# More seven-product pairs in two feed-forward networks, and late ones in their first groups

## The chip, the cores and the metric

The kernel runs on one core of a Trainium2 chip. The metric is the device time of one execution in microseconds (us), lower is better. TensorE (PE in the profile) does matrix products, VectorE (DVE) and ScalarE (ACT) elementwise work, GpSimd (POOL) and SyncE (SP) issue most of the transfers; all of them run their own instructions in order and wait for each other by semaphores.

## The reference

Two transformer blocks for 256 tokens of width 2048, all in float32. Both end in a feed-forward network (FFN), and only these are touched:

```
# block 1: gated, FFN_HIDDEN = 5632
gate, up = split(h @ w_ffn_in)            # 2048 -> 2 x 5632
x = x + rms_norm((silu(gate) * up) @ w_ffn_out, g)
# block 2: squared relu, D_FF = 8192
f = square(relu(x @ w_ff1)) @ w_ff2       # 2048 -> 8192 -> 2048
x = layer_norm(alpha * x + f, g, b)
```

## The kernel before

Every float32 operand is used as two parts, a rounded one (`h` for weights, `H` for activations) and the rest (`l`, `L`). A product of two tiles is three matmuls: high by high, high by low, low by high. Weights stream from memory in halves of 128 x 1024 (SyncE issues the loads, up to five ahead). For each half ScalarE copies it into the rounded part (L253) and VectorE subtracts to get the rest (L254); the pair of tiles (h, l) is one *unit*. Five units fit in the pool, and `Stream.half` asks for the splits four units ahead of TensorE's use. So the split of a unit waits until TensorE has finished the unit five before it.

The contraction over 2048 rows goes in eight *pairs* of 2 x 128 rows. In the first FFN product of both blocks (all but the opening step, `i0`) `Prog.seven` computes a group of 256 tokens x 1024 columns at a time, four blocks of 128 tokens x 512 columns. A string of eight letters says how each pair is done:

- an **N** pair does the eight tile products directly: two units, 24 matmuls into four accumulators `c`;
- an **S** pair does seven products (Strassen-Winograd): four units, 21 matmuls into `c` and four further accumulators `m`. It needs sums of weight tiles, which `splitting4` makes on VectorE (L275, L277, L278) with four splits (L272 on ScalarE, L279 on VectorE), and sums of token tiles, made once per FFN by `seven_gen` beside the opening step.

Before the first S pair of a group takes its accumulators, all delayed work (`late`: transposes and splits of earlier results) is issued at once. After the last S pair ScalarE and VectorE combine `m` into the shared sums (L644 to L651), one part after each of the next two units; at the end of the group L655 adds `c`, and the activation follows: in block 1 L1719 and L1721 (silu, and the product of gate and up), in block 2 L1964 and L1965. The results are then transposed on TensorE (L1750) and split into the hidden operand (L665, L666). These transposes are delayed by one or more units.

The steps run in a fixed order. In block 1 step `i0` is a plain product, `i1`, `i2`, `i3` and `i5` consist of two groups one right behind the other, `i4` of one: nine groups. Where two groups follow each other, the second has its `c` in the banks that the first used for `m`, and the reverse. In block 2 `i1` to `i7` are one group each: seven groups. Between them stand the steps `o`, the second FFN product (L506 to L508). Each `o` step handles the hidden part made one `i` step earlier; `i1` directly follows `i0`.

PSUM is held as two pools: `pa` (three banks) and `pb` (five). In block 2 a group has its `c` in `pb`, three of its `m` in `pa` and one in `pb`, so one bank of `pb` is free for transposes until the first S pair. The `o` step accumulates in `pa`.

The lines named by the prediction: L606 to L608 are the three matmuls of `prod` in `seven`; L506 to L508 those of `rowsmm`; L579 to L584 the token sums.

Of the kernel before, what the change touches and what calls it, by code (L numbers as in the profile page):

```python
# [23 lines left out]
FFN = 5632  # L24
# [13 lines left out]
FF_PARTS = (8,) * 8  # L38
SEQ_GLU = "NSNNSNNN"
SEQ_FF = "NSNSNSNN"  # L40
MID = 64 + 2 + 128
# [34 lines left out]
def _fours():  # L76

    at = lambda i, seq: [i + 2 * p for p, s in enumerate(seq) if s == "S"]
    u, n = [], 0
    for step in FFN_ORDER:  # L80
        nt = FFN_PARTS[int(step[1:])]
        if step[0] == "i" and step != "i0":
            for b in range(nt // 4):
                u += at(n + 16 * b, SEQ_GLU)
        n += 4 * nt if step[0] == "i" else 2 * nt
    n += MID
    for step in FF_ORDER:
        if step[0] == "i" and step != "i0":
            u += at(n, SEQ_FF)
        n += 16  # L90
    return [i - n for i in u]


def _weights(a):
    w_in, w_out = a["w_in"][0], a["w_out"][0]
    w_ckv, w_fi, w_fo = a["w_ckv"][0], a["w_ffn_in"][0], a["w_ffn_out"][0]
# [13 lines left out]
    for step in FFN_ORDER:  # L110
        p = int(step[1:])
        lo, hi = int(starts[p]), int(starts[p + 1])
        if step[0] == "o":
            u.append(_rows(w_fo[lo * 128:hi * 128]))
        elif p == 0:
            u.append(gate_up[lo // 4:hi // 4].reshape(-1, 128, 2048))
        else:
            for b in range(lo * 128, hi * 128, 512):
                u.append(_seven(np.concatenate([w_fi[:, i + b:i + b + 512] for i in (0, FFN)], axis=1), SEQ_GLU))
    u += [  # L120
# [10 lines left out]
    for step in FF_ORDER:  # L131
        p = int(step[1:])
        lo, hi = int(starts[p]), int(starts[p + 1])
        if step[0] == "o":
            u.append(_rows(w2[lo * 128:hi * 128]))
        else:
            u.append(_seven(w1[:, lo * 128:hi * 128], SEQ_FF) if p else _rows(w1[:, lo * 128:hi * 128]))
    w = np.concatenate(u, axis=0)
# [185 lines left out]
class Prog:  # L324
# [243 lines left out]
    def seven_gen(self, xp, seq, st):  # L568


        nc = self.nc
        for i, p in enumerate(p for p, s in enumerate(seq) if s == "S"):
            yield 1.9
            if i % 2 == 0:
                t = self.slot([128, 2, 2, 4, 128], "seven", F32R)
            w = self.t4([128, 2, 4, 128], "s7")
            a = w[:, 0].rearrange("p (k x) t -> p k (x t)", k=2)
            s = w[:, 1]
            nc.vector.tensor_tensor(a, xp.H(2 * p, 2).bitcast(F32), xp.L(2 * p, 2).bitcast(F32), OP.add)  # L579
            a11, a21, a12, a22 = a[:, 0, :128], a[:, 0, 128:], a[:, 1, :128], a[:, 1, 128:]  # L580
            nc.vector.scalar_tensor_tensor(out=s[:, 0], in0=a21, scalar=-1.0, in1=a22, op0=OP.mult, op1=OP.subtract)
            nc.vector.scalar_tensor_tensor(out=s[:, 1], in0=s[:, 0], scalar=-1.0, in1=a11, op0=OP.mult, op1=OP.subtract)
            nc.vector.tensor_tensor(s[:, 2], a11, a21, OP.subtract)
            nc.vector.tensor_tensor(s[:, 3], a12, s[:, 1], OP.subtract)  # L584
            yield 0.7
            self.split2(s, t[:, i % 2, 0], t[:, i % 2, 1])
            st.append(t[:, i % 2])

    def seven(self, xp, seq, st, out, swap=False):
# [22 lines left out]

        si = 0
        for p, s in enumerate(seq):
            if s == "N":
# [7 lines left out]
                continue  # L623
            if si == 0:
                while self.late:
                    self.settle()
                m = {i: f() for i, f in zip((5, 7, 6, 1), more)}
            sum_ = lambda i: (st[si][:, 0, i], st[si][:, 1, i])
            cut = lambda i: slice(512 * i, 512 * i + 512)
# [7 lines left out]
            self.tick()  # L637
            si += 1
            if not end:
# [1031 lines left out]
    def ffn(self):  # L1671
# [4 lines left out]
        hid = {}  # L1676
        g = self.row(2)
        ss = self.cp.tile([128, 2, 8], F32, tag="ss", name="ss2")
        sv, st, after_swap = [], [], False
        last = len(FFN_PARTS) - 1  # L1680
        for step in FFN_ORDER:
            p = int(step[1:])
            nt = FFN_PARTS[p]
            if step[0] == "i":
                hid[p] = Pair(self, "hid", nt)
                if p == 0:
                    self.rowsmm(hT, 16, nt // 2, self.ev_glu(hid[p]), lag=4, begin=lambda: sv.append(self.start(self.seven_gen(hT, SEQ_GLU, st))))
                    continue
                self.drain(sv[0])
                for b in range(nt // 4):  # L1690
                    self.seven(hT, SEQ_GLU, st, self.glu(hid[p], b), swap=b % 2 == 1)
                after_swap = nt == 8
                continue
            if p == last:
                self.xT = Pair(self, "xT2", 16)
# [239 lines left out]
    def ff2(self):  # L1935
        nc, x = self.nc, self.x
        hT = self.hT

        hid, sg, st = {}, [], []
        self.bn = self.cp.tile([128, 2, 8, 6], F32, tag="bn", name="bn1")  # L1940
        last = len(FF_PARTS) - 1
        for step in FF_ORDER:
            p = int(step[1:])
            nt = FF_PARTS[p]
            if step[0] == "i":
# [11 lines left out]
                if p == 0:  # L1957
                    self.rowsmm(hT, 16, nt // 4, ev, lag=4, begin=lambda: sg.append(self.start(self.seven_gen(hT, SEQ_FF, st))))
                    continue
# [8 lines left out]

                self.seven(hT, SEQ_FF, st, relu2)
                continue  # L1970
# [78 lines left out]
```

## Time and profile before

| | |
|---|---|
| median of three runs | 2594.05 us (2592.15 to 2597.99) |
| the profiled execution: its time | 2596.54 us |
| its span in the trace | 2594.8 us |
| TensorE busy, matmuls | 2561.9 us, 12936 |
| VectorE busy | 1786.2 us |
| ScalarE busy | 1325.9 us |
| mean granted TensorE clock | 0.995 |
| seven-product groups of block 1 | 677 to 1241 us, with the `o` steps between |
| seven-product groups of block 2 | 1924 to 2492 us, with the `o` steps between |

In a row of a timeline the first number is the start and the second the duration, both in us, then engine, line and operation, what is written and read, and the number of instructions merged into the row. A bracket at the end is the idle time of that engine just before, with the instruction that ended it. Matmuls overlap each other: a duration of 0.39 us is not the distance between two starts.

### The profile page before, as it was taken

The page shows a single profiled execution, that of the slowest core. Times are in us where ns is not written, and L with a number is a line of the kernel's source. Part 1 is how long each engine was busy: PE and PEld are TensorE (multiplying, and loading weights), DVE is VectorE, ACT ScalarE, POOL GpSimd, SP SyncE. Part 2 cuts the span into 40 slices and gives each one's busy share as a digit, 9 for nine tenths or more (in the row PEclk, how much of TensorE's full clock was granted, in tenths as well). Part 3 has the DMA queues.
Part 4 walks back from the last instruction along what each step waited for, and adds up shares of the span by engine and source line. Part 5 has one row for each costly group of instructions (what it writes and reads, how often), then busy time and mean ns, then how long its engine had stood idle before and what let it go on. Part 6 is the DMA issues. An engine that isn't in the chain of part 4 may idle for free. (4 is left out here: it accounts for less than half of the span.)

```text
span 2594.8 us, 33924 instructions
## 1 busy us (share of the span) xinstructions
PE 2561.9 (99%) x12936; PEld 2171.5 (84%) x12936; DVE 1786.2 (69%) x2270; ACT 1325.9 (51%) x1777; POOL 62.4 (2%) x59
## 2 busy tenths in 40 slices
PE   9999999999999999999999999999999999999998
PEld 8989888988888888888888888888778888888886
DVE  5766857766676767668676764456677776777676
ACT  6533667656455545445444464444445544554553
POOL 0000000110000000000010000000100000000001
PEclk9999999999999999999999999999999999999999
DMA  7544557555555556556555655565456555655663
GB/s 283 179 153 142 176 178 247 196 177 174 192 194 191 198 194 197 194 177 212 188 182 184 208 171 187 195 223 182 152 167 210 195 194 179 205 198 187 216 208 122
DMA packets 134083, 493.34 MB, mean 190 GB/s; under 512 B 15149, under 2 KB 15541, under 8 KB 131744
## 3 DMA queue, kind: packets, MB, share of 16 engines
q1 hardware_dynamic: 129888, 470.34, 53.9%
q0 software_dynamic: 2880, 17.76, 2.1%
q10 hardware_dynamic: 1152, 3.07, 0.3%
q8 instruction: 101, 1.65, 0.3%
q14 instruction: 62, 0.51, 0.1%
HBM read 486.91 MB, written 2.11 MB: 188 GB/s over the span
## 5 line engine op out<-in xcount | busy, mean ns | idle before, releaser
L254 DVE TENSOR_TENSOR l<-w,h 128x1024 fp32r<-128x1024 f32 (+1 forms) x802 | 975.3, 1223 | 669.6 <-ACT h L253 659.0
L253 ACT ACTIVATE h<-w 128x1024 fp32r<-128x1024 f32 (+1 forms) x805 | 844.9, 1058 | 752.0 <-PE pa L508 442.0
L506 PE MATMUL pa<-h,hid 128*128 128x512 f32 (+1 forms) x808 | 316.4, 392 | 0.0
L508 PE MATMUL pa<-h,hid 128*128 128x512 f32 (+1 forms) x808 | 313.1, 388 | 0.0
L507 PE MATMUL pa<-l,hid 128*128 128x512 f32 (+1 forms) x808 | 312.7, 387 | 0.0
L606 PE MATMUL pb<-h,hT 128*128 128x512 f32 x669 | 260.9, 390 | 2.8 <-DVE hid L666 2.8
L608 PE MATMUL pb<-h,hT 128*128 128x512 f32 x669 | 260.5, 389 | 0.0
L607 PE MATMUL pb<-l,hT 128*128 128x512 f32 x669 | 260.4, 389 | 0.0
L506 PE MATMUL pa<-h,xT 128*128 128x512 f32 x500 | 201.6, 403 | 2.5 <-ACT ghg L935 1.3
L508 PE MATMUL pa<-h,xT 128*128 128x512 f32 x500 | 195.7, 391 | 0.0
L507 PE MATMUL pa<-l,xT 128*128 128x512 f32 x500 | 195.5, 391 | 0.0
L508 PEld LDWEIGHTS pa<-h,hid 128*128 128x128 f32 x808 | 151.7, 188 | 31.4
L507 PEld LDWEIGHTS pa<-l,hid 128*128 128x128 f32 x808 | 151.9, 188 | 30.1
L506 PEld LDWEIGHTS pa<-h,hid 128*128 128x128 f32 x808 | 151.8, 188 | 29.7
L606 PEld LDWEIGHTS pb<-h,hT 128*128 128x128 f32 x669 | 125.6, 188 | 28.9 <-DVE hid L666 3.3
L608 PEld LDWEIGHTS pb<-h,hT 128*128 128x128 f32 x669 | 125.6, 188 | 26.2
L607 PEld LDWEIGHTS pb<-l,hT 128*128 128x128 f32 x669 | 125.6, 188 | 25.9
L463 PE MATMUL pa<-xT,h 128*128 128x256 f32 x496 | 142.8, 288 | 1.0 <-ACT xT L685 0.9
L465 PE MATMUL pa<-xT,l 128*128 128x256 f32 x496 | 141.2, 285 | 1.0 <-DVE l L254 1.0
L464 PE MATMUL pa<-xT,h 128*128 128x256 f32 x496 | 141.4, 285 | 0.1
L459 PE MATMUL pa<-xT,h 128*128 128x512 f32 x384 | 134.0, 398 | 0.0
L506 PEld LDWEIGHTS pa<-h,xT 128*128 128x128 f32 x500 | 94.4, 189 | 25.3 <-issue 2.7
(507 smaller groups left out, 4569.6 us busy)
## 6 DMA issues: line engine op xcount, KB each, us to landing
w<-W SPq DMA_DIRECT2D x889, 512.0 KB, 3.5
row<-rows POOLq DMA_DIRECT2D x7, 1024.0 KB, 7.1
xn<-x ACTq DMA_DIRECT2D x2, 1024.0 KB, 8.6
mn<-mem POOLq DMA_DIRECT2D x2, 1024.0 KB, 6.0
memraw<-memT POOLq DMA_DIRECT2D x2, 1024.0 KB, 6.7
x<-x POOLq DMA_DIRECT2D x2, 1024.0 KB, 7.2
xraw<-xT SPq DMA_DIRECT2D x3, 512.0 KB, 8.5
out<-x SPq DMA_DIRECT2D x6, 256.0 KB, 2.5
```

The costliest lines, as they stand in the source:

```text
L253: nc.scalar.activation(out=h[:, s], in_=t[:, s], func=AF.Copy)
L254: (nc.gpsimd if j in self.slow else nc.vector).tensor_tensor(l[:, s], t[:, s], h[:, s].bitcast(F32), OP.subtract)
L459: mm(o, h[:, k], xp.both(kt), start=kt == 0, stop=kt == nkt - 1)
L463: mm(o, h[:, k], xp.H(kt), start=kt == 0, stop=False)
L464: mm(o, h[:, k], xp.L(kt), start=False, stop=False)
L465: mm(o, l[:, k], xp.H(kt), start=False, stop=kt == nkt - 1)
L506: mm(o, xh, h[:, k, c], start=kt == 0, stop=False)
L507: mm(o, xh, l[:, k, c], start=False, stop=False)
L508: mm(o, xl, h[:, k, c], start=False, stop=kt == nkt - 1)
L606: mm(o, ah, wh, start=first, stop=False)
L607: mm(o, ah, wl, start=False, stop=False)
L608: mm(o, al, wh, start=False, stop=end)
```

## The change

The strings become tables with an entry for the first group of an FFN and one for the others. Block 1: `NSNNSNNN` becomes `NSNSNSNN`, and `NNNSNSNN` in the first group. Block 2: `NSNSNSNN` becomes `SNSNSNSN`, and `NNNNSNSN` in the first group. Token sums are kept by the number of their pair (a first group uses some of them only), three pairs in block 1 and four in block 2, where there were two and three. The packing of the weights follows the strings. In block 1 the third tile for token sums takes a slot of 8 KB a partition, and the load of the row `g` (POOL's queue) moves from the start of the FFN to step `o4`.

```diff
-SEQ_GLU = "NSNNSNNN"
-SEQ_FF = "NSNSNSNN"
+SEQ_GLU = {"first": "NNNSNSNN", "": "NSNSNSNN"}
+SEQ_FF = {"first": "NNNNSNSN", "": "SNSNSNSN"}
 ...
     def seven_gen(self, xp, seq, st):
 ...
-            st.append(t[:, i % 2])
+            st[p] = t[:, i % 2]
 ...
     def seven(self, xp, seq, st, out, swap=False):
 ...
-            if si == 0:
+            if not m:
                 while self.late:
                     self.settle()
                 m = {i: f() for i, f in zip((5, 7, 6, 1), more)}
-            sum_ = lambda i: (st[si][:, 0, i], st[si][:, 1, i])
+            sum_ = lambda i: (st[p][:, 0, i], st[p][:, 1, i])
 ...
     def ffn(self):
 ...
-        g = self.row(2)
 ...
                 for b in range(nt // 4):
-                    self.seven(hT, SEQ_GLU, st, self.glu(hid[p], b), swap=b % 2 == 1)
+                    self.seven(hT, SEQ_GLU["first" if p == 1 and b == 0 else ""], st, self.glu(hid[p], b), swap=b % 2 == 1)
 ...
+            if p == last - 1:
+                g = self.row(2)
 ...
     def ff2(self):
 ...
-                self.seven(hT, SEQ_FF, st, relu2)
+                self.seven(hT, SEQ_FF["first" if p == 1 else ""], st, relu2)
```

In the new file the lines of `Stream` up to L600 or so are two further down and those behind `seven` one further (L254 becomes L256, L1750 becomes L1751); L644 to L655 keep their numbers.

What moves, in the order in which the engines run it. TensorE at the first group of block 2, before: behind the first N pair's last matmul both blocks of transposes (`ident,sq`, results of the opening product) stand back to back, and the S pair (its operand `seven` are the token sums) follows.

```order
L608 MATMUL pb_16443<-h_16377,hT_891_15307 128x512
L1750 MATMUL pb_16478<-ident,sq_16434 128x128 x4
L1750 MATMUL pb_16485<-ident,sq_16436 128x128 x4
L606 MATMUL pb_16495<-h_16395,hT_891_15307 128x512
L607 MATMUL pb_16495<-l_16396,hT_891_15307 128x512
L608 MATMUL pb_16495<-h_16395,hT_891_15307 128x512
L606 MATMUL pb_16441<-h_16395,seven_16185 128x512
```

TensorE at the same place after the change, around the second block of transposes (the first stands twelve matmuls ahead):

```order
L608 MATMUL pb_16536<-h_16484,hT_909_15396 128x512
L609 MATMUL pb_16536<-l_16485,hT_909_15396 128x512
L610 MATMUL pb_16536<-h_16484,hT_909_15396 128x512
L1751 MATMUL pb_16601<-ident,sq_16522 128x128 x4
L608 MATMUL pb_16535<-h_16504,hT_909_15396 128x512
L609 MATMUL pb_16535<-l_16505,hT_909_15396 128x512
```

The two blocks now lie a unit apart and have matmuls of N pairs on both sides.

VectorE between the two groups of step `i2` in block 1, before: the shared sums (L645 to L651) with the splits of the next group's N pair among and behind them, then the first sum of weights for its S pair (L275).

```order
L645 TENSOR_TENSOR u_499_7846<-pa_7678,u_498_7845 128x512
L646 TENSOR_TENSOR u_500_7847<-pa_7676,u_499_7846 128x512
L254 TENSOR_TENSOR l_7873<-w_7812,h_7872 128x1024
L650 TENSOR_TENSOR u_499_7846<-pa_7677,u_499_7846 128x512
L651 TENSOR_TENSOR u_501_7848<-pa_7676,u_499_7846 128x512
L254 TENSOR_TENSOR l_7893<-w_7824,h_7892 128x1024
L254 TENSOR_TENSOR l_7911<-w_7836,h_7910 128x1024
L275 TENSOR_TENSOR s_7930<-w_7849,w_7870 128x1024
```

VectorE at the same place after the change:

```order
L645 TENSOR_TENSOR u_504_7909<-pa_7695,u_503_7908 128x512
L646 TENSOR_TENSOR u_505_7910<-pa_7693,u_504_7909 128x512
L256 TENSOR_TENSOR l_7936<-w_7875,h_7935 128x1024
L650 TENSOR_TENSOR u_504_7909<-pa_7694,u_504_7909 128x512
L651 TENSOR_TENSOR u_506_7911<-pa_7693,u_504_7909 128x512
L277 TENSOR_TENSOR s_7957<-w_7887,w_7899 128x1024
```

The shared sums stand two splits later, directly ahead of the S pair's weight sums.

VectorE at the end of a group in block 2 reads the same before and after (five splits, L645, L646, a split, L650, L651, then the splits of the next step), but two of the five splits belonged to the second N pair behind the last S pair, and now belong to the next `o` step.

More of the change, by code (lines that the diff above doesn't have):

```diff
@@ L76, in _fours @@
 def _fours():
+    first = lambda c: "first" if c else ""
     at = lambda i, seq: [i + 2 * p for p, s in enumerate(seq) if s == "S"]
@@ L83, in _fours @@
             for b in range(nt // 4):
-                u += at(n + 16 * b, SEQ_GLU)
+                u += at(n + 16 * b, SEQ_GLU[first(step == "i1" and b == 0)])
         n += 4 * nt if step[0] == "i" else 2 * nt
@@ L88, in _fours @@
         if step[0] == "i" and step != "i0":
-            u += at(n, SEQ_FF)
+            u += at(n, SEQ_FF[first(step == "i1")])
         n += 16
@@ L118, in _weights @@
             for b in range(lo * 128, hi * 128, 512):
-                u.append(_seven(np.concatenate([w_fi[:, i + b:i + b + 512] for i in (0, FFN)], axis=1), SEQ_GLU))
+                s = SEQ_GLU["first" if b == lo * 128 and p == 1 else ""]
+                u.append(_seven(np.concatenate([w_fi[:, i + b:i + b + 512] for i in (0, FFN)], axis=1), s))
     u += [
@@ L136, in _weights @@
         else:
-            u.append(_seven(w1[:, lo * 128:hi * 128], SEQ_FF) if p else _rows(w1[:, lo * 128:hi * 128]))
+            u.append(_seven(w1[:, lo * 128:hi * 128], SEQ_FF["first" if p == 1 else ""]) if p else _rows(w1[:, lo * 128:hi * 128]))
     w = np.concatenate(u, axis=0)
@@ L611, in tok @@
             return tuple(f(kt, 1, tb * 128, tb * 128 + 128) for f in (xp.H, xp.L))
-        si = 0
         for p, s in enumerate(seq):
@@ L637, in seven @@
             self.tick()
-            si += 1
             if not end:
@@ L1676, in ffn @@
         hid = {}
-        g = self.row(2)
         ss = self.cp.tile([128, 2, 8], F32, tag="ss", name="ss2")
-        sv, st, after_swap = [], [], False
+        sv, st, after_swap = [], {}, False
         last = len(FFN_PARTS) - 1
@@ L1686, in ffn @@
                 if p == 0:
-                    self.rowsmm(hT, 16, nt // 2, self.ev_glu(hid[p]), lag=4, begin=lambda: sv.append(self.start(self.seven_gen(hT, SEQ_GLU, st))))
+                    self.rowsmm(hT, 16, nt // 2, self.ev_glu(hid[p]), lag=4, begin=lambda: sv.append(self.start(self.seven_gen(hT, SEQ_GLU[""], st))))
                     continue
@@ L1937, in ff2 @@
         hT = self.hT
-        hid, sg, st = {}, [], []
+        hid, sg, st = {}, [], {}
         self.bn = self.cp.tile([128, 2, 8, 6], F32, tag="bn", name="bn1")
@@ L1957, in ff2 @@
                 if p == 0:
-                    self.rowsmm(hT, 16, nt // 4, ev, lag=4, begin=lambda: sg.append(self.start(self.seven_gen(hT, SEQ_FF, st))))
+                    self.rowsmm(hT, 16, nt // 4, ev, lag=4, begin=lambda: sg.append(self.start(self.seven_gen(hT, SEQ_FF[""], st))))
                     continue
```

## The prediction, made before the changed kernel ran

> **What bounds the kernel now.** I read the page's head first, then TensorE's rows in order of time, then the stretches of time by group, and last VectorE's rows around the edited pairs.
>
> ```profile
> span 2594.8 us, 33924 instructions
> PE 2561.9 (99%) x12936; PEld 2171.5 (84%) x12936; DVE 1786.2 (69%) x2270; ACT 1325.9 (51%) x1777; POOL 62.4 (2%) x59
> L606 PE MATMUL pb<-h,hT 128*128 128x512 f32 x669 | 260.9, 390 | 2.8 <-DVE hid L666 2.8
> row<-rows POOLq DMA_DIRECT2D x7, 1024.0 KB, 7.1
> ```
>
> TensorE is busy for 99% of the span, so a matmul that disappears is worth time only if TensorE is truly fed there. The 390 ns of the matmul's row is not that worth: matmuls overlap. The price is the distance between starts. These are the first matmuls of an S pair, of the S pair two pairs later, and of the N pair behind it, in block 2's second seven-product group:
>
> ```profile
> 2021.82 0.39 PE L606 MATMUL pb<-h,hT 128*128 128x512 f32 x1
> ...
> 2032.02 0.39 PE L606 MATMUL pb<-h,hT 128*128 128x512 f32 x1
> ...
> 2036.78 0.39 PE L606 MATMUL pb<-h,hT 128*128 128x512 f32 x1
> ```
>
> From 2021.82 to 2032.02 TensorE issues one S pair (21 matmuls) and one N pair (24): 10.20 us / 45 = 0.2267 us a matmul. The S pair alone takes 2036.78 - 2032.02 = 4.76 us = 21 x 0.2267, an N pair 10.20 - 4.76 = 5.44 us. Nothing is lost between matmuls. Priced by the row's mean the change would look 1.7 times as large.
>
> The groups as stretches (TensorE, weight load, VectorE, ScalarE, POOL, clock, DMA share, GB/s):
>
> ```profile
> 677.10:764.90 87.80, 86.39 (x389) 71.41 (x388) 65.90 (x70) 44.34 (x48) 0.00 (x0) 1.00 0.56 193
> 939.10:1024.30 85.20, 85.20 (x381) 70.63 (x381) 64.53 (x68) 43.39 (x46) 0.00 (x0) 1.00 0.60 199
> ...
> 1923.60:1970.90 47.30, 44.47 (x193) 36.34 (x192) 34.94 (x38) 23.79 (x26) 0.00 (x0) 0.96 0.54 184
> 2016.30:2057.80 41.50, 41.50 (x185) 34.37 (x184) 33.32 (x35) 22.23 (x23) 0.00 (x0) 1.00 0.61 208
> 2450.90:2492.40 41.50, 41.50 (x185) 34.35 (x183) 33.33 (x35) 22.24 (x23) 0.53 (x1) 1.00 0.71 242
> ```
>
> Rows two, four and five are ordinary: a double gate/up group (85.2 us) and single groups of block 2 (41.5 us), TensorE without a gap. Rows one and three are the first group of each FFN; they alone hold idle TensorE time (1.4 and 2.8 us), and row three has a clock of 0.96.
>
> **The change part by part.** *Matmuls removed.* Gate/up has nine groups. The first keeps two S pairs, the other eight go from two to three. Block 2 has seven: the first goes from three to two, six from three to four. That is 8 + 6 - 1 = 13 more S pairs, 39 fewer matmuls; the built program has just 39 fewer rows on TensorE. 39 x 0.2267 = 8.84 us less, if the operands arrive in time.
>
> *VectorE's added work.* It must hide behind TensorE. One N pair, one S pair, the end of a group on VectorE, and the first matmul of the output product behind it:
>
> ```profile
> 2033.37 2.58 DVE L254 TENSOR_TENSOR l<-w,h 128x1024 fp32r<-128x1024 f32 x2 [0.97 <-ACT h L253]
> 2035.87 1.22 DVE L275 TENSOR_TENSOR s<-w,w 128x1024 f32<-128x1024 f32 x1
> ...
> 2041.91 0.69 DVE L279 TENSOR_TENSOR l<-w,h 128x512 fp32r<-128x512 f32 x1
> 2043.57 6.39 DVE L254 TENSOR_TENSOR l<-w,h 128x1024 fp32r<-128x1024 f32 x5 [0.98 <-ACT h L253]
> 2049.88 0.69 DVE L645 TENSOR_TENSOR u<-pa,u 128x512 f32<-128x512 f32 x1
> ...
> 2052.37 0.68 DVE L650 TENSOR_TENSOR u<-pa,u 128x512 f32<-128x512 f32 x1
> 2053.09 0.69 DVE L651 TENSOR_TENSOR u<-pa,u 128x512 f32<-128x512 f32 x1
> ...
> 2057.86 0.39 PE L506 MATMUL pa<-h,hid 128*128 128x512 f32 x1
> ```
>
> An S pair costs VectorE 2035.87 to 2042.60 = 6.73 us, an N pair 2.58. So 4.15 us are added per exchanged pair. Inside an S pair VectorE is slower than TensorE (6.73 against 4.76); over S and N together it needs 9.31 of 10.20, and each N pair still begins with 0.97 or 0.98 us of waiting for ScalarE. The units of 2033.37 (N pair four) are ready at 2034.6, 2.2 us before their use at 2036.78, and the same distance follows one period later. So the alternation keeps its lead, and block 2's new groups only prolong an alternation that this trace already runs. By groups: single ones get 33.32 + 4.15 = 37.5 us of VectorE in 40.8; double gate/up ones 64.53 + 8.30 = 72.8 in 83.8. Cost on the path: 0; if the cover went, 2 us per S pair (rivals).
>
> *Sums of tokens for the new pairs* (one pair more in each FFN). One pair's sums on VectorE stand in block 2's opening product:
>
> ```profile
> 1915.28 0.69 DVE L579 TENSOR_TENSOR s<-hT 128x512 f32<-128x512 f32 x1
> ...
> 1916.74 0.28 DVE L584 TENSOR_TENSOR s<-s 128x128 f32<-128x128 f32 x1
> ...
> 1920.68 0.69 DVE L666 TENSOR_TENSOR seven<-s,seven 128x512 fp32r<-128x512 f32 x1
> ```
>
> About 2.4 us each. In block 2 the fourth falls at the first group's start, where VectorE loses an S pair's 6.73 us (it moves two pairs later). Cost 0.
>
> *First groups, S pairs late.* An S pair first drains the delayed work, so the transposes of the opening product are issued back to back and wait for each other's bank:
>
> ```profile
> 683.04 0.60 PE L1750 MATMUL pb<-ident,sg 128*128 128x128 f32 x4
> 685.05 0.50 PE L606 MATMUL pb<-h,hT 128*128 128x512 f32 x1 [1.41 <-DVE hid L666]
> ...
> 1929.12 0.60 PE L1750 MATMUL pb<-ident,sq 128*128 128x128 f32 x4
> 1931.13 0.66 PE L1750 MATMUL pb<-ident,sq 128*128 128x128 f32 x4 [1.41 <-DVE hid L666]
> 1933.20 0.50 PE L606 MATMUL pb<-h,hT 128*128 128x512 f32 x1 [1.41 <-DVE hid L666]
> ...
> 1933.85 0.63 PE L608 MATMUL pb<-h,hT 128*128 128x512 f32 x1
> ...
> 1936.83 0.51 PE L606 MATMUL pa<-h,seven 128*128 128x512 f32 x1
> ```
>
> A block of four transposes takes 0.60 us with its tail and moves the next start by 0.44 (eight take 1.03, in a row below). Gate/up: 2.01 - 0.44 = 1.6 us. Block 2: 1933.20 - 1929.12 - 0.88 = 3.2 us of waits. Then seven steps from 1933.85 to 1936.83 take 2.98 us in place of 1.59: half clock, 1.4 us, plus 0.2 at the restart. With three or four N pairs first, the delayed work drains by itself, with 12 matmuls (2.72 us) between the blocks in block 2. In between, a ScalarE and a VectorE operation must empty the one free bank behind an ordinary split; I allow 0.1 us of waiting there. Gain 1.6 + 4.7 = 6.3 us; its bounds are 4.2 (the three bracketed waits alone) and 6.6 (the two long stretches against the ordinary ones, 2.6 and 5.8, less two blocks each).
>
> The Trainium skill, page "TensorE: Matmul & The Clock Gate", section on HAM oscillation, gives as the rule that only idle gaps over some 3.4 us throttle the clock. By that rule the half-clock steps would not come from these two waits and would stay, and the gain would be 4.9 us. The trace speaks against it: the waits here are 1.41 us each, and the slow steps begin 0.65 us behind the second.
>
> *Between the two halves of a double gate/up group* (four places). The last S pair moves one pair later, so the shared sums L645 to L651 end 4.1 us before the second half (as in block 2: 2053.78 against the N pair's end at 2057.86), not 9.6 as now (842.05 against 851.61). They now stand directly ahead of the second half's S pair on VectorE, where two N splits stood between. The rows before:
>
> ```profile
> 841.36 0.69 DVE L651 TENSOR_TENSOR u<-pa,u 128x512 f32<-128x512 f32 x1
> ...
> 851.61 0.39 PE L606 MATMUL pa<-h,hT 128*128 128x512 f32 x1
> ...
> 851.38 2.48 DVE L655 TENSOR_TENSOR u<-pb,u 128x512 f32<-128x512 f32 x4
> 853.77 1.22 DVE L279 TENSOR_TENSOR l<-t,h 128x1024 fp32r<-128x1024 f32 x1
> ...
> 856.17 0.74 DVE L1721 SCALAR_TENSOR_TENSOR u<-u,rxx,u 128x512 f32<-128x512 f32 x1
> 857.06 1.03 PE L1750 MATMUL pb<-ident,u 128*128 128x128 f32 x8
> ```
>
> The second L1721 ends at 856.91; its transposes are the second four of the eight, at 857.06 + 0.43 = 857.49: 0.58 us to spare. Carrying the later sums through VectorE's order, with ScalarE's splits where they are, moves L655 from 851.38 to 852.2 and the second L1721 by the same 0.8 us, to 857.7. TensorE then waits some 0.3 us: 4 x 0.3 = 1.2 us. Bounds 0 and 4 x 0.8.
>
> *End of a group in block 2* (seven places). Only one N pair now follows the last S pair. The sums end at the same distance from that pair: L645 at 2050.57, 3.6 us behind its end at 2046.98 (one period behind 2036.78); L650 at 2053.05, 6.1 behind; L651 6.8 behind. The output product begins 5.44 us behind it. In the built program its first accumulator waits for L645 and its second, needed six matmuls later at 6.80, for L650. Spare 0.7 us; cost 0, bound 1.4 us each (were it L651 at once).
>
> *Moved row load.* The gain row goes from the FFN's start to the last output product but one, 85 us ahead of its use against 7.1 us of landing; two such loads lie in the 2450.90 stretch, which is still 41.50 us. Weights: the same 16 loads in 40.8 us, 2% more rate than 208 GB/s. POOL has nothing queued behind it that is due. Cost 0.
>
> Sum: - 8.84 - 6.3 + 1.2 = - 13.9 us. The profiled execution took 2596.54 us, 2.5 above the median 2594.05. So 2582.6 for it and 2580 us as median.
>
> **Rivals.** *B, the accumulators.* The sums at block 2's group ends come 0.7 us or more later than the old rows say (VectorE carries 4 us more per group), and each output product starts with a wait. At 1.4 us, seven of them give back 9.8 us: 2590 us, within 0.2% of before (5.2 us, about what a measurement of this kernel can tell from no change). For it: a margin of 0.7. Against it: the same five splits stand ahead of L645 in both orders.
>
> *C, VectorE becomes the bound* and the kernel gets slower. Place: every S pair of the alternating groups. Price: 6.73 - 4.76 = 2.0 us for each. It decides once S and N cost VectorE over 10.20 us, 0.9 more than the 9.31 measured. All 48 S pairs outside the first groups would cost 96 us; the 13 new ones alone 26, that is 2606 us. Against it: the lead of 2.2 us repeats.
>
> *D, the first groups keep their loss*, since the waits move to the transposes' new places or the last sums: 2580 + 6 = 2586 us. Against it: two full steps of 2.72 us between them. A variant: the half clock of 1933.85 does not come from the waits and stays, at 1.4 us: 2581.4 us. The page of the Trainium skill named above states the rule that would do this.
>
> **How the numbers follow.** Forecast 0.72, D 0.10 (of it 0.03 the clock variant), B 0.11, C 0.07. Low end: all gains, no new wait, from the lowest run: 2592.15 - 15.1 = 2577. High end: B's 2590. Outside lie C and part of the rest, under 2 in 10. Faster by over 0.2% (below 2588.9): forecast and D and a partial B, 0.86; within: 0.08; slower: 0.06.
>
> **What would show it.** The stretches: double gate/up groups near 84.1 us (85.2 less six matmuls, plus 0.3), single groups of block 2 near 40.8, the first ones near 86 and 43. The clock is 1.00 in block 2's first group, and TensorE's waits there are gone. L666 as releaser ahead of the seven-product matmuls disappears; the multiplication of gate and up as releaser of the transposes appears, four times some 0.3 us. Wrong would be: waits of TensorE for weight splits inside S pairs (C), or for L650 and L651 at the output products (B).

## The result and the profile after

The changed kernel took 2580.16 us (median of four runs, 2578.79 to 2585.18) against 2596.02 us for the kernel before (four runs, 2592.15 to 2599.46): ratio 0.9941, 95% interval 0.9928 to 0.9954. A second set of five runs, on another chip, gave 2581.6 against 2596.59: 0.9940, 0.9926 to 0.9954. The forecast was 2580, range 2577 to 2590.

The head of the page and the rows that answer to those of before:

```profile
span 2583.4 us, 33968 instructions
PE 2552.8 (99%) x12897; PEld 2164.4 (84%) x12897; DVE 1840.9 (71%) x2347; ACT 1347.3 (52%) x1805; POOL 62.4 (2%) x59
L608 PE MATMUL pb<-h,hT 128*128 128x512 f32 x620 | 241.9, 390 | 0.0
```

TensorE ran 39 matmuls fewer, VectorE is busy for 55 us longer, and the idle time ahead of the seven-product matmuls (2.8 us before) is gone. The stretches (TensorE, weight load, VectorE, ScalarE, POOL, clock, DMA share, GB/s): block 1's first double group, an ordinary double gate/up group, block 2's first group, and two single groups of block 2.

```profile
679.80:765.60 85.80, 85.72 (x387) 70.76 (x386) 72.02 (x78) 46.08 (x50) 0.00 (x0) 1.00 0.58 196
810.10:894.20 84.10, 84.02 (x375) 69.49 (x374) 71.36 (x76) 47.17 (x51) 0.00 (x0) 1.00 0.61 202
...
1920.50:1963.70 43.20, 43.20 (x196) 35.61 (x195) 33.58 (x39) 22.61 (x25) 0.00 (x0) 1.00 0.56 177
2008.10:2048.90 40.80, 40.80 (x182) 33.79 (x181) 35.70 (x37) 24.22 (x25) 0.00 (x0) 1.00 0.63 207
2438.50:2479.30 40.80, 40.80 (x182) 33.80 (x181) 35.55 (x37) 23.95 (x25) 0.53 (x1) 1.00 0.71 235
```

These are the stretches forecast (86, 84.1, 43, 40.8), with a clock of 1.00 in block 2's first group, where it was 0.96. TensorE sat idle there for 2.8 us; now it has no gap. The two blocks of transposes stand apart:

```profile
1925.91 0.60 PE L1751 MATMUL pb<-ident,sq 128*128 128x128 f32 x4
1926.26 0.48 PE L608 MATMUL pb<-h,hT 128*128 128x512 f32 x1
...
1929.13 0.66 PE L1751 MATMUL pb<-ident,sq 128*128 128x128 f32 x4
1929.55 0.47 PE L608 MATMUL pb<-h,hT 128*128 128x512 f32 x1
```

No bracket stands behind either block: the free bank is emptied while 12 matmuls of an N pair run.

Between the halves of a double group, where 0.3 us of waiting was forecast, VectorE and then TensorE read:

```profile
837.25 6.39 DVE L256 TENSOR_TENSOR l<-w,h 128x1024 fp32r<-128x1024 f32 x5 [0.98 <-ACT h L255]
...
846.73 0.69 DVE L651 TENSOR_TENSOR u<-pa,u 128x512 f32<-128x512 f32 x1
...
856.87 0.74 DVE L1722 SCALAR_TENSOR_TENSOR u<-u,rxx,u 128x512 f32<-128x512 f32 x1
```

```profile
856.99 1.33 PE L1751 MATMUL pb<-ident,u 128*128 128x128 f32 x8
858.08 0.48 PE L608 MATMUL pb<-h,hT 128*128 128x512 f32 x1
```

The second L1722 ends at 857.61, too late for the second four transposes, which would be due at 857.42. The row of eight therefore takes 1.33 us where it took 1.03 before. VectorE has no idle time from 837.25 to 857.61.

Summed by block, from the start of the first seven-product matmul to the start of the last matmul of the second FFN product: block 1 went from 633.01 to 627.18 us (-5.83), block 2 from 657.86 to 649.73 (-8.13), in all -13.96. The profiled executions differ by less (2596.54 to 2585.18, 11.4 us), since the part ahead of the first edited group took 2.62 us longer in the one after; that part is untouched and takes 675.0 to 680.4 us in the traces of this study. So the stretches, not one execution's total, carry the verdicts below.

### The profile page after: what moved, and what is told of

Read it like the earlier page. It is cut to its first block, busy times and chain, and to the rows that moved or that the text cites. A ratio compares the mean times of both kernels' runs of the same rounds, so it can differ in the third digit from the quotient of the medians.

```text
span 2583.4 us, 33968 instructions
## 1 busy us (share of the span) xinstructions
PE 2552.8 (99%) x12897; PEld 2164.4 (84%) x12897; DVE 1840.9 (71%) x2347; ACT 1347.3 (52%) x1805; POOL 62.4 (2%) x59
## 5 line engine op out<-in xcount | busy, mean ns | idle before, releaser
L256 DVE TENSOR_TENSOR l<-w,h 128x1024 fp32r<-128x1024 f32 (+1 forms) x776 | 942.7, 1222 | 611.7 <-ACT h L255 601.3
L255 ACT ACTIVATE h<-w 128x1024 fp32r<-128x1024 f32 (+1 forms) x779 | 816.4, 1057 | 694.3 <-PE pa L510 437.5
L608 PE MATMUL pb<-h,hT 128*128 128x512 f32 x620 | 241.9, 390 | 0.0
L610 PE MATMUL pb<-h,hT 128*128 128x512 f32 x620 | 241.3, 389 | 0.0
L609 PE MATMUL pb<-l,hT 128*128 128x512 f32 x620 | 241.2, 389 | 0.0
L610 PEld LDWEIGHTS pb<-h,hT 128*128 128x128 f32 x620 | 116.4, 188 | 24.2
L608 PEld LDWEIGHTS pb<-h,hT 128*128 128x128 f32 x620 | 116.4, 188 | 23.9
L609 PEld LDWEIGHTS pb<-l,hT 128*128 128x128 f32 x620 | 116.4, 188 | 23.8
L274 ACT ACTIVATE h<-w 128x1024 fp32r<-128x1024 f32 x104 | 87.5, 841 | 59.5 <-PE pa L510 26.5
```

The costliest lines, as they stand in the source:

```text
L255: nc.scalar.activation(out=h[:, s], in_=t[:, s], func=AF.Copy)
L256: (nc.gpsimd if j in self.slow else nc.vector).tensor_tensor(l[:, s], t[:, s], h[:, s].bitcast(F32), OP.subtract)
L608: mm(o, ah, wh, start=first, stop=False)
L609: mm(o, ah, wl, start=False, stop=False)
L610: mm(o, al, wh, start=False, stop=end)
```

## The experiments

All start from the changed kernel; its lines shift by up to four where an edit adds some. "Block 1" and "block 2" are the stretches just defined (627.18 and 649.73 us after the change). The first expectations end block 1's stretch 7.3 us earlier, inside the second FFN product (625.65 us before, 619.86 after), so for block 1 their differences compare with the measured ones, and their totals do not.

**late_only.** The old strings, except in the first groups: there the S pairs come late and are one fewer in each block. This is the second half of the change without the first.

```diff
-SEQ_GLU = {"first": "NNNSNSNN", "": "NSNSNSNN"}
-SEQ_FF = {"first": "NNNNSNSN", "": "SNSNSNSN"}
+SEQ_GLU = {"first": "NNNNSNNN", "": "NSNNSNNN"}
+SEQ_FF = {"first": "NNNSNSNN", "": "NSNSNSNN"}
```

> Only the first groups differ from the kernel before: NNNNSNNN in block 1 (one S pair, was two) and NNNSNSNN in block 2 (two, was three); all other groups keep the old strings. Stretches are taken from the first seven-product matmul of a block to the last matmul of its second FFN product: 625.65 us and 657.86 us before, 619.86 and 649.73 after the change. Theory (late S pairs take away the waits and the half clock): 625.65 - 1.6 + 0.68 = 624.7 us and 657.86 - 4.7 + 0.68 = 653.8 us, in all 4.9 us less than before, and no stretch of half clock near the first group of block 2. Rival (the loss only moves to another place): 626.3 and 658.5 us. Rival by the idle-gap rule (half clock stays): 624.7 and 655.2 us.

Measured: 2591.11 us, ratio 0.9977 (0.9967 to 0.9987). Block 2's first group took 43.13 us, not 47.27, with no half-clock stretch; all other groups of both blocks kept the length they had before the change. Block 1: 631.98 (-1.03 against the kernel before), block 2: 653.71 (-4.15), each with one S pair fewer.

```profile
1922.60:1965.70 43.10, 43.10 (x195) 35.62 (x194) 32.89 (x35) 22.09 (x24) 0.00 (x0) 1.00 0.57 193
```

So the waits and the slow clock of the first groups are worth what was forecast: they come from an S pair standing early, and go with it. The S pair that is missing costs 3 x 0.2267 = 0.68 us in each block, which makes 1.7 and 4.8 us against 1.6 and 4.7 forecast.

**early_first.** The reverse: all new S pairs, the first groups like the others.

```diff
-SEQ_GLU = {"first": "NNNSNSNN", "": "NSNSNSNN"}
-SEQ_FF = {"first": "NNNNSNSN", "": "SNSNSNSN"}
+SEQ_GLU = {"first": "NSNSNSNN", "": "NSNSNSNN"}
+SEQ_FF = {"first": "SNSNSNSN", "": "SNSNSNSN"}
```

> As the changed kernel, but the first groups use the same string as the others (NSNSNSNN and SNSNSNSN), so that their first S pairs come early and there is one S pair more in block 1 and two more in block 2. Theory: block 1 gets the old wait back and saves three matmuls: 619.86 + 1.6 - 0.68 = 620.8 us. Block 2 drains the delayed work before its very first matmul: square, transposes, split, transposes, split, at 1.6 us a step beyond the first and with a stretch of half clock (1.4 us), 5 to 8 us in all less 1.36 for six matmuls: 649.73 + 4 to 7 = 654 to 657 us. Rival (the forced drain cost little, the gain came from elsewhere): 619.2 and 648.4 us.

Measured: 2587.99 us, ratio 0.9964 (0.9951 to 0.9977). Block 1's first group came out as expected (86.79 against 85.83, with one wait of 1.4 us for L666). Block 2 missed: its stretch fell to 647.45, and a wait moved ahead of it, net 1.2 us worse than after instead of 4 to 7. (The medians lie 7.8 us apart, and the two blocks make 2.2 of it. The opening part, which no edit touches, took 680.35 us in this trace, the longest of all.)

```profile
1924.51 1.23 PE L1751 MATMUL pb<-ident,sq 128*128 128x128 f32 x8 [2.62 <-DVE sq L1954]
1925.50 0.47 PE L608 MATMUL pb<-h,hT 128*128 128x512 f32 x1
```

With the S pair first, the group has written none of its accumulators when the delayed work is drained, and both blocks of transposes run as one row of eight without waiting for each other's bank. There is one wait, 2.62 us for the squares of the opening product, and no half clock behind it. Two S pairs more give back 1.36 us. An early S pair is thus not bad in itself: an S pair in second place, with one bank left, is.

**first_third.** The first S pair of block 2's first group in third place.

```diff
-SEQ_FF = {"first": "NNNNSNSN", "": "SNSNSNSN"}
+SEQ_FF = {"first": "NNSNSNSN", "": "SNSNSNSN"}
```

> As the changed kernel, but the first group of block 2 is NNSNSNSN: three S pairs in place of two, the first of them directly behind the two N pairs that the delayed work needs. Theory: the drain is done by then (one unit of 2.72 us for each of its four steps), so only three matmuls go: 649.73 - 0.68 = 649.05 us for block 2, block 1 unchanged at 619.86. Rival (the drain needs more than two pairs): a wait ahead of that S pair, 650 to 652 us.

Measured: 2581.63 us, ratio 0.9947 (0.9932 to 0.9962); block 2 651.16, the first group 44.65. The S pair more saves 0.68 us of matmuls, and the stretch still grew by 1.43, as the rival said. TensorE, VectorE and ScalarE:

```profile
1921.42 0.63 PE L1751 MATMUL pb<-ident,sq 128*128 128x128 f32 x4 [0.32 <-DVE sq L1954]
...
1926.30 0.66 PE L1751 MATMUL pb<-ident,sq 128*128 128x128 f32 x4 [1.48 <-DVE hid L666]
```

```profile
1923.12 1.22 DVE L281 TENSOR_TENSOR l<-s,h 128x1024 fp32r<-128x1024 f32 x1
1924.41 1.22 DVE L281 TENSOR_TENSOR l<-t,h 128x1024 fp32r<-128x1024 f32 x1
1925.56 0.68 DVE L666 TENSOR_TENSOR hid<-pb,hid 128x512 fp32r<-128x512 f32 x1
```

```profile
1923.32 1.06 ACT L274 ACTIVATE h<-t 128x1024 fp32r<-128x1024 f32 x1 [2.60 <-DVE t L280]
1924.29 0.58 ACT L665 ACTIVATE hid<-pb 128x512 fp32r<-128x512 f32 x1
```

12 matmuls stand between the two blocks, as after the change, but they do not cover: L665 and L666, which empty the bank, stand behind the S pair's own sums and splits on both engines. ScalarE sits idle for 2.60 us until VectorE's sum L280 is there, makes the split L274, and only then starts L665, 2.24 us behind the end of the first block (1922.05); VectorE has one more split ahead of L666. The prediction's "two full steps between them" is only enough because the S pair's work on these two engines is also two pairs away.

**sums_later.** Two more VectorE operations of 0.69 us ahead of L645 at the end of block 2's groups, to measure the room that rival B doubted.

```diff
+                for _ in range(2 if last_s == 6 else 0):
+                    nc.vector.tensor_tensor(u[5], m[6], u[1], OP.add)
```

> As the changed kernel, with two more VectorE operations of 128x512 (as L645, into a tile that is written anew later) ahead of L645 at the seven group ends of block 2, so L650 ends about 1.35 us later. Theory (0.7 us to spare for the second accumulator): a wait of 0.6 to 0.7 us ahead of the seventh matmul of each output product, 7 x 0.65 = 4.5 us: block 2 at 654.2 us. Rival (the accumulators have more room, or VectorE catches up): 649.7 us. Rival (no room at all): 649.73 + 9.5 = 659.2 us.

Measured: 2587.39 us, ratio 0.9967 (0.9956 to 0.9978), block 2 655.00 (+5.27), 0.75 a group; all of it at the output products:

```profile
PE pa L508 <- DVE u L652: 3.2, 7, 0.5
```

```profile
2049.04 0.39 PE L508 MATMUL pa<-h,hid 128*128 128x512 f32 x1
...
2050.28 0.68 DVE L652 TENSOR_TENSOR u<-pa,u 128x512 f32<-128x512 f32 x1
```

(The columns of the first line: us in total, times, longest; L652 is L650 here. The list counts 0.46 us a time; the rest of the 0.75 is lost at the restart, where matmuls do not overlap.) L652 ends 1.92 us behind the start of the output product. In the changed kernel L650 ends 0.59 behind it:

```profile
2049.83 0.68 DVE L650 TENSOR_TENSOR u<-pa,u 128x512 f32<-128x512 f32 x1
```

It ends at 2050.51; the output product starts at 2049.92 and needs it six matmuls later, at 2051.28. Delayed by 1.92 - 0.59 = 1.33 us, the groups lose 0.75, so the room is 0.58 us, close to the 0.7 read from the old trace. Rival B was real and one operation of VectorE away.

**one_more** and **three_more.** One and three more VectorE operations in each S pair (S + N then 10.0 and 11.4 us against the 10.20 of TensorE): rival C's threshold from both sides.

```diff
-            nc.vector.tensor_tensor(t[:, lo], a[:, hi], s[:, lo], OP.add)
+            for _ in range(2):       # three_more: range(4)
+                nc.vector.tensor_tensor(t[:, lo], a[:, hi], s[:, lo], OP.add)
```

> As the changed kernel, but each S pair of both blocks has one VectorE operation of 128x512 more (L279's sum is made twice, 0.69 us). S and N pair then need 2.58 + 6.73 + 0.69 = 10.0 us of VectorE, TensorE 10.20. Theory (VectorE bounds only above 10.20): groups of block 2 stay at 40.80 us; in block 1 the activation between two groups comes up to 0.7 us later, 84.2 to 84.9 us. Rival (VectorE already sets the pace of the S pairs): 0.69 us for each S pair, 43.6 us a group of block 2.

> As one_more with three operations: S and N pair need 11.4 us of VectorE against TensorE's 10.20. Theory: TensorE waits for weight splits from the second or third S pair of a group on; VectorE needs some 36.7 us from 2.2 us behind the group's start until the last N pair's units are ready, where TensorE wants the first of them at 35.4 us: 3.5 us and more a group (44 to 45 us), then 1 to 2 us for the shared sums at the output product: block 2 at 670 to 685 us. Rival (the lead of one group and the slack of the output product carry even that): 41 us a group.

Measured: with one more, 2584.32 us (one run); block 2 unchanged (649.68, groups 40.80), double gate/up groups 84.89. With three more, 2616.87 us (one run); block 2 664.18 with groups of 41.8 to 42.5, double groups 88.9 to 89.4. The waits, first of one_more, then of three_more:

```profile
PE pb L1752 <- DVE u L1723: 2.4, 4, 0.6
```

```profile
PE pb L1752 <- DVE u L1723: 11.6, 7, 2.7
PE pa L509 <- DVE u L651: 5.0, 7, 1.8
PE pa L610 <- DVE l L282: 3.4, 6, 0.6
```

Rival C's threshold, put at 10.20, lies between these two values: S + N of 10.0 costs block 2 nothing, at 11.4 the kernel is slower than before. The price beyond was overestimated (44 to 45 us a group expected): the alternation is only four periods long and its lead is used up first, so waits for weight splits inside block 2's groups (L282) are 3.4 us in all, and the ends of groups pay more. In block 1 (the waits for L1723) four windows of half clock follow such waits, at 729, 862, 996 and 1217 us.

**glu_adjacent.** Block 1's second and third S pairs side by side, so that the shared sums come one N pair earlier.

```diff
-SEQ_GLU = {"first": "NNNSNSNN", "": "NSNSNSNN"}
+SEQ_GLU = {"first": "NNNSSNNN", "": "NSNSSNNN"}
```

> As the changed kernel, but block 1 uses NSNSSNNN (NNNSSNNN in its first group): the same number of S pairs, the last one at the place that it had before the change (three N pairs behind it), at the price of two S pairs side by side. Theory (the later shared sums push the activation behind the end of the second group's first N pair): the 0.3 us a place is gone, double gate/up groups go from 84.17 to 83.87 us, and VectorE's lead falls to some 0.8 us inside the second of the adjacent S pairs but not to zero, so no wait of TensorE appears. Rival (adjacent S pairs run TensorE dry): waits for weight splits inside the second S pair, 84.5 us or more; single group of block 1 over 41.48 us.

Measured: 2582.0 us, ratio 0.9948 (0.9932 to 0.9965), not to be told from after; but the double groups take 83.85 us in place of 84.17, block 1 625.85 (-1.33): the wait between the halves is gone, and the second S pair's units are still ready 0.7 us or more before use.

**sums_at_once.** The same wait attacked in another way: the shared sums are issued one unit earlier, the first half (L644 to L646) straight behind the last S pair, the second (L650, L651) one unit behind that.

```diff
-            self.later(shared1)
+            shared1()
```

> The kernel after the change, but the second half of a group's shared sums (L648 to L651) is written straight behind the group's last S pair instead of being handed on to be written one unit of work later. Theory: the 0.24 us wait between the two halves of a double gate/up group is VectorE's queue order (L655 and L1722 stand behind the later sums). Written earlier, the sums leave before the splits of the next N pair, and the wait goes: double groups 83.9 us in place of 84.17, block 2's groups unchanged at 40.80, its stretch 649.7; in all 1.3 us less, about 2579. Rival: the order in which the sums are written does not matter, since VectorE is held by the ScalarE split ahead of it: double groups stay 84.17.

Measured: 2584.39 us (one run), block 1 627.09, double groups 84.16: the theory fell, the rival held. VectorE:

```profile
844.95 0.69 DVE L651 TENSOR_TENSOR u<-pa,u 128x512 f32<-128x512 f32 x1
...
856.22 0.74 DVE L1722 SCALAR_TENSOR_TENSOR u<-u,rxx,u 128x512 f32<-128x512 f32 x1
```

This execution is 0.62 us ahead here (its first group starts at 679.13, the other's at 679.75). L651 runs 846.73 - 844.95 - 0.62 = 1.16 us earlier, and L1722 0.03 us. VectorE is without idle time either way, so the work in between fills the place: what counts is the sum of work on VectorE since its last idle time at 837, not the order inside it. In glu_adjacent the same stretch holds idle time of VectorE (1.29, 0.36 and 0.22 us), and there the wait is gone. In one_more it holds one operation of 0.69 us more, and the double groups are 0.72 us longer.

**five** and **five_at_once.** Five S pairs in block 2, without and with the early sums; the second also leaves the token sums that the opening product has not finished until the first S pair needs them.

```diff
-SEQ_FF = {"first": "NNNNSNSN", "": "SNSNSNSN"}
+SEQ_FF = {"first": "NNNSNNSN", "": "SNSSNSSN"}      # five
+SEQ_FF = {"first": "NNNNNSSN", "": "SNSSNSSN"}      # five_at_once, and
-            self.later(shared1)
+            shared1()
-                self.drain(sg[0])
+                self.waiting = sg                   # drained in seven, ahead of its first S pair
```

> As the changed kernel, but block 2 uses SNSSNSSN: five S pairs of eight in six groups (first group NNNSNNSN, two as in the changed kernel). Theory (VectorE needs 6.73 us for an S pair that TensorE does in 4.76, and a lead of 2 to 4 us carries one adjacent pair but not a second one): some 0.4 us of waiting in the last S pair, 40.80 - 0.68 + 0.4 = 40.5 us a group, and the shared sums come 1.7 us later behind it, a wait of 1.0 us at each output product (room 0.65): block 2 at 649.73 + 6 x 0.8 = 654.5 us, slower than with four. Rival (the lead is enough, three matmuls fewer are worth their 0.68 us each time): 649.73 - 4.1 = 645.6 us.

> Five S pairs of eight in block 2 (SNSSNSSN), the sums written straight behind the last S pair, and in the first group (NNNNNSSN) the token sums that are left over are issued only ahead of the first S pair. Theory: the 0.75 us waits at the output products of the variant with five S pairs came from L650 standing behind the splits of the last N pair; 1.1 to 1.4 us earlier it ends 6.4 to 6.7 us behind the last S pair against a need at 6.80, so the waits vanish: groups 40.12 us, each output product without a wait, first group about 43.2, block 2's stretch 649.7 - 4.1 = 645.6. Rival: VectorE has no room left with five S pairs, so its whole queue runs later and the waits stay near 0.7 us at each output product: 650 us or more, no gain over four S pairs.

Measured: five 2590.73 us, block 2 656.15; five_at_once 2577.54 us, block 2 645.73 (one run each). Of the 6.4 us that five's block 2 lost, 4.0 are the first group's (47.20 us), which the theory did not have: there VectorE makes the token sums of the last two pairs (1918.79 to 1924.97) ahead of the squares (L1954) that the transposes wait for. The six others lost 0.4 each, half of what it gave them. Five had no wait inside its groups (40.12 us), but these, at the output products and in the first group:

```profile
PE pa L508 <- DVE u L650: 3.7, 5, 1.0
PE pb L1751 <- DVE sq L1954: 2.6, 1, 2.6
PE pb L1751 <- DVE hid L666: 1.1, 1, 1.1
PE pa L508 <- DVE u L645: 0.6, 1, 0.6
```

On VectorE ahead of an output product (five, then five_at_once, where L652 is L650):

```profile
2050.72 0.69 DVE L646 TENSOR_TENSOR u<-pa,u 128x512 f32<-128x512 f32 x1
2052.11 1.22 DVE L256 TENSOR_TENSOR l<-w,h 128x1024 fp32r<-128x1024 f32 x1 [0.71 <-ACT h L255]
2053.26 0.68 DVE L650 TENSOR_TENSOR u<-pa,u 128x512 f32<-128x512 f32 x1
```

```profile
2043.15 0.69 DVE L648 TENSOR_TENSOR u<-pa,u 128x512 f32<-128x512 f32 x1
2043.76 1.22 DVE L256 TENSOR_TENSOR l<-w,h 128x1024 fp32r<-128x1024 f32 x1
2044.89 0.68 DVE L652 TENSOR_TENSOR u<-pa,u 128x512 f32<-128x512 f32 x1
```

The output products start at 2051.77 and 2045.36. In five L650 ends 2.17 us after the start, 0.8 behind the seventh matmul's time (1.36); in five_at_once its counterpart ends 0.21 after the start. Here issuing the sums earlier does help, since the product waits for the sum itself, and in five a split that waits for ScalarE (0.71 us) stood ahead of it. Block 2 then came out at 645.73, where 645.6 was expected.

**dense.** All of it: block 2 as in five_at_once, block 1 with adjacent S pairs, and a fourth one in the last group of each step, behind which no second half waits.

```diff
-SEQ_GLU = {"first": "NNNSNSNN", "": "NSNSNSNN"}
+SEQ_GLU = {"first": "NNNSSNNN", "": "NSNSSNNN", "end": "NSNSSNSN"}
+glu_key = lambda p, b: "first" if (p, b) == (1, 0) else "end" if b == FFN_PARTS[p] // 4 - 1 else ""
...
-                    self.seven(hT, SEQ_GLU["first" if p == 1 and b == 0 else ""], st, self.glu(hid[p], b), swap=b % 2 == 1)
+                    self.seven(hT, SEQ_GLU[glu_key(p, b)], st, self.glu(hid[p], b), swap=b % 2 == 1)
```

> All that the runs so far suggest together: block 2 as in the variant with five S pairs and early sums; gate/up with its S pairs adjacent (NSNSSNNN, first group NNNSSNNN), and four S pairs (NSNSSNSN) in the last group of each gate/up step, behind which no second half waits for VectorE. Theory: less 1.3 us (no wait between halves), less 5 x 0.68 = 3.4 us (three matmuls fewer in five groups), less 4.1 us in block 2: 2580.2 - 8.8 = about 2571 us, ratio to the kernel before 0.990 to 0.991. Rival: VectorE is full at the ends of groups, the sums of tokens and weights come late, and the waits give back the matmuls: 2578 to 2584, ratio 0.993 to 0.995, no better than the kernel after the change.

Measured: 2575.51 us (five runs, 2572.79 to 2577.52), ratio 0.9924 (0.9911 to 0.9938). This lies between the theory (2571) and the rival (2578 or more). Block 2 645.73 as expected; block 1 623.41 (-3.77 of -4.7 expected). The groups did give 4.65 us, but the five stretches of `o` steps behind them took 0.17 us more each (four of them 44.66 in place of 44.49, the last 69.88 in place of 69.71), 0.9 in all, with waits too short for the list:

```profile
895.25 0.75 DVE L1725 SCALAR_TENSOR_TENSOR u<-u,rxx,u 128x512 f32<-128x512 f32 x1
```

```profile
895.70 0.39 PE L512 MATMUL pb<-h,hid 128*128 128x512 f32 x1
896.05 0.66 PE L1754 MATMUL pb<-ident,u 128*128 128x128 f32 x4
```

The transposes start 0.35 us behind the matmul ahead of them instead of 0.23, since L1725 ends at 896.00: the same wait as between the halves, in a new place. VectorE is nearly full here, in block 2 quite:

```profile
2005.00:2045.10 40.10, 40.10 (x179) 33.20 (x178) 39.45 (x42) 25.32 (x27) 0.00 (x0) 1.00 0.61 205
```

39.45 of 40.1 us: a sixth S pair, 4.15 us more by the prediction's rows, finds no room on this engine.

**after_again.** The changed kernel unedited, since the medians of dense and after were 4.65 us apart where their stretches say 7.8.

> The kernel after the change once more, unedited, so that the dense variant (2575.51 us) is compared with a second set of runs of it. By the traces' stretches the two differ by 4.0 us in block 1's network and 4.25 us in block 2's, 8.3 us in all, while the medians so far are 4.65 us apart. Theory: the stretch ahead of the first edited group, 675 to 680 us long from run to run, makes the difference; its median over all traces is 677.6, so this kernel should come out near 677.6 + 627.2 + 613.5 + 649.7 + 13.2 + 1.8 = 2583 us, 7 to 8 above the dense variant. Rival: 2580 is its time, and the dense variant is worth only 4 to 5 us.

(The 4.0 and 4.25 us of this expectation end dense's stretches two matmuls early; they are 3.8 and 4.0.)

Measured: 2581.6 us (2579.48 to 2583.69), between theory and rival. The slowest of dense's five runs (2577.52) is faster than the fastest of nine of the changed kernel (2578.79), so dense beats both kernels. By how much beside after stays open between 5.3 (2575.51 against 2580.78, the median of the nine) and 8.05 us (its profiled execution against 2583.56 for this one, of which the stretches give 7.67).

## Why the prediction was right

*Price of a matmul.* Right. 0.2267 us each: every plain group lost just 0.68 us per S pair (41.48 to 40.80 us). Priced by the row's mean of 390 ns the 39 matmuls would have been 15.2 us.

*VectorE's work costs nothing.* Right, and its limit is bracketed: at 10.0 of 10.20 us a pair of pairs (one_more) block 2 still loses nothing, at 11.4 it does. The work itself came as forecast (54.7 us for 13 pairs, 4.2 each), though a single group holds 35.70 us of it and not 37.5, since its first S pair's work is done in the `o` step before. Rival C had the right point but the wrong place: it charged the S pairs, and in three_more TensorE waited 3.4 us inside them and 11.6 + 5.0 us at the ends of groups. Its 2606 us was worked out for another load than that of three_more (2616.87) and is not confirmed.

*First groups, 6.3 us.* Right: 1.7 + 4.8 in late_only, and in the changed kernel block 2's first group fell from 47.27 to 43.21 us with one S pair fewer (4.06 + 0.68 = 4.74). The half clock was part of it: it went with the waits, in late_only too, so the variant of rival D that kept it (2581.4) is ruled out. That variant went by the rule in the Trainium skill's page "TensorE: Matmul & The Clock Gate", section on HAM oscillation. Whether each execution of the kernel before has this half clock, its one trace does not show; by the last section it depends on where the windows fall. The allowance of 0.1 us for the free bank was not needed. But the reason given was incomplete: first_third keeps 12 matmuls between the blocks and waits 1.48 us, since ScalarE and VectorE must also be free of the S pair's work by then.

*Between the halves, 1.2 us.* The size was right (84.17 - 83.85 = 0.32 us, four times, 1.3 in all), the mechanism was not. The prediction put it on the later place of the sums in VectorE's order; sums_at_once moved L651 1.16 us earlier, and nothing changed. It is VectorE's load between 837 and 857 us. The number probably came out because carrying the order forward counted the same load: it gave 857.7 for the end of L1722, measured 857.61. (From 857.7 against 857.49 its own rows give a wait of 0.2 us; it wrote 0.3.)

*Ends of block 2's groups, 0, room 0.7 us.* Right: no wait, and sums_later measures 0.58. So B's chance of 0.11 was not idle: one VectorE operation more at that place and the price begins.

*The sum.* -13.9 forecast, -13.96 in the stretches: 8.84 for the matmuls, 4.74 and 1.66 for the first groups (87.85 - 85.83 of block 1's first double group, less 0.68 for matmuls, plus the 0.32 that it waits between its halves), less 1.28 between the halves. Between the medians it is -15.9; the scatter from the untouched opening part (5 us) is larger than that gap. That 2580 was hit to 0.2 us is luck: the forecast started from 2594.05, 2 us below the 2596.02 of the four runs, and the medians then fell 2 us further than forecast. That the stretches agree term by term is not luck.

## What to carry over

Price a removed matmul by the distance between starts, then follow, on the engine that takes over the work, its last idle time ahead of each deadline: with no idle time in between it is the total load since then that decides, and reordering inside it helps only the operation that is itself waited for. Before an operation is put early in a stage, see what must be drained ahead of it and how many buffers are free then; second place with one free bank was the worst of those tried. Where a change moves less than the scatter of an untouched part, judge it by stretches between the same instructions.

## What the runs showed of the hardware

*The slow clock follows 3.413 us windows, and a window need not be idle throughout.* Two neighbouring windows of the kernel before:

```profile
1930.20:1933.61 3.41, 1.06 (x6) 0.79 (x7) 1.59 (x3) 1.70 (x3) 0.00 (x0) 1.00 0.30 109
1933.61:1937.02 3.41, 3.41 (x10) 2.63 (x9) 1.11 (x2) 1.06 (x1) 0.00 (x0) 0.51 0.36 137
```

Between the first 20 us of a run and its last stage, the half-clock stretches last 3.413 us or twice that, and start on one grid of 3.413 us per execution. Here the last 0.88 us of one wait of 1.41 us and the whole of the next make 2.3 us of idle time in one window, and the next window runs at half clock. The windows ahead of the other half-clock stretches there that follow idle time hold 1.8 to 2.6 us of it; those with 1.7 us or less were followed by full clock, and between 1.8 and 1.95 both happened. The wait of 2.62 us in early_first did nothing: it fell across two windows, 1.0 and 1.6 us. In three_more single waits with 2.4 and 2.6 us inside one window were followed by half clock. The Trainium skill's page "TensorE: Matmul & The Clock Gate" gives, in its section on HAM oscillation, one gap over some 3.4 us as the rule. These runs disagree. By the same page of the Trainium skill, section "A second HAM failure mode: psum-queue depth-cycling", frequent short pauses between groups of matmuls slow the clock too. That fits these runs; the section gives no bound.

*Matmuls with few columns seem to count as idle.* The opening part is half-clocked in some executions at about 172 and 238 us, with no idle time ahead:

```profile
234.39:237.80 3.41, 3.41 (x34) 3.41 (x32) 3.41 (x5) 1.06 (x1) 0.00 (x0) 1.00 0.70 239
237.80:241.21 3.41, 3.41 (x18) 3.41 (x18) 0.08 (x1) 0.00 (x0) 0.00 (x0) 0.50 0.47 159
```

```profile
236.11 0.41 PE L1264 MATMUL pb<-qt,f 128*128 128x64 f32 x2
236.36 0.33 PE L1266 MATMUL pb<-ones,E 128*128 128x1 f32 x2
```

The window before consists of matmuls of 64 columns and of one. Such a run of small matmuls at 168 us is 3.6 us long, hardly longer than a window, so whether one window holds little else depends on the grid. Five of the fourteen traces have no slow stretch at either place and reach the first edited group after 675.0 to 677.3 us; the seven with both need 677.1 to 680.4. That is the likely source of the scatter between runs; it was not tested by an edit.

*Counted in columns, both cases are one.* Take every full-clock window of the grid between the first 20 us and the last stage, in all fourteen traces, and add up the columns of the matmuls that start in it; 512-column matmuls without a gap make 7,680. Of the 37 windows with under 2,330 columns 36 were followed by half clock (22 of the 37 hold over 1 us of idle time, 15 none), of the 24 with 2,330 to 3,340 columns 9 were, and of the 10,343 with more none.
